# The substitution steps of a chunked gated DeltaNet issued from GpSimd, and the first heads' gated rows issued two ticks later

## The chip, the cores and the metric

The kernel runs on one core of one Trainium2 chip. A core has a matrix engine (TensorE, PE in the profile), VectorE (DVE), ScalarE (ACT), GpSimd (POOL) and SyncE (SP), which here only issues DMA transfers. Each engine takes its instructions in the order in which they were queued for it, and waits for the others by semaphores. The metric is the device time of one execution in microseconds (us), of which the median over several runs is given. All data are float32.

## The reference

Two layers of a hybrid decoder for 256 tokens of width 1024: a half feed-forward block, a token mixer, a cross-attention into 256 memory tokens, another half feed-forward block. In the first layer the mixer is attention beside a linear recurrence; in the second, to which the change belongs, it is a chunked gated delta rule with 8 heads of width 128. Cut to what matters:

```python
def gated_delta_rule_chunked(q, k, v, g, beta):
    ...
    kkt = einsum('bhnid,bhnjd->bhnij', k * beta[..., None], k) * decay
    amat = eye(C) + where(strict, kkt, 0.0)
    rhs = concatenate([v * beta[..., None], k * beta[..., None] * exp(gcum)[..., None]], axis=-1)
    sol = triangular_solve(amat, rhs, left_side=True, lower=True, unit_diagonal=True)
    ...
    o = rmsnorm(o, o_norm) * silu(z)
    return o.reshape(B, S, W) @ w_out
```

So for every head and chunk of tokens a unit lower triangular system is solved, and the rows of the result are normalised and gated by silu(z) before the output projection.

## The kernel before

The activations lie transposed in SBUF: 8 tiles of 128 features x 256 tokens. Every weight tile is loaded by SP (`raw`, L141, 512 KB, five buffers), copied by ACT (L158) and its rounding rest formed by DVE (L159); the pair of halves, `wt`, is what PE multiplies, in two passes (L200 and L204, or L216 and L220 where tokens are the rows of the result). The products gather in PSUM banks named psw (3), pss (3) and psf (2). DVE and ACT bring them out: `add` (L270 on ACT, L271 on DVE) gives `xn` or `z`.

In `mixer1` the order of the projections is DN_ORDER: keys, queries, values and gates of the four pairs of heads (k0, q0, v0, z0 and so on). Each projected pair goes through a convolution of four taps (L1078, and three L1081 on DVE), a SiLU and its own further steps. Small pieces of work are hung into the sequence by `after(n, fn)`: they are emitted n ticks later, a tick being about a quarter of a projection. This fixes the order of the program as it is written. From it a list scheduler with its own estimates of the durations makes the queue of each engine; it may let a later instruction pass an earlier one, and it keeps the data dependences. So the place of an instruction in a queue follows from what the scheduler expects of the time of the others.

The kernel solves the triangular system by inverting it. The 128 x 128 matrix of a head and chunk of 128 tokens (`na`, L1176, on DVE) is stored to DRAM (L1180), and its 16 x 16 diagonal blocks are read back with one block per partition (`nb`, L1235): 64 blocks for the two pairs of one group. There are two groups: heads 0 to 3 and heads 4 to 7. `invert(g)` then does the substitution inside the blocks, in 15 steps of two instructions:

```python
def step(j):
    n, m = 15 - j, j + 1
    nc.vector.tensor_mul(tm[:, :n, :m], nb[:, j, m:, None]..., ti[:, 0, j:m, :m]...)   # L1240
    nc.vector.tensor_add(ti[:, 0, m:, :m], ti[:, 0, m:, :m], tm[:, :n, :m])            # L1242
    if j == 14:
        nc.vector.tensor_copy(ti[:, 1], ti[:, 0].rearrange("p a b -> p b a"))          # L1244
```

A step works on 64 partitions and (15-j) x (j+1) elements of each, 15 to 64. Each instruction needs the one before it. `ti[:, 0]` and its transpose `ti[:, 1]` are stored (L1248, SP) and loaded again as 128 x 128 matrices `tu` (L1254, SP). `tu`, `nb` and `ti` have one buffer each, shared by the two groups. `back(p)` goes on from the blocks of 16 to 128 by products on PE (L1275, L1281, L1287), with a masked copy on DVE in each of three rounds (L1282), and then computes the result of the head pair. `gated(p)` multiplies the result by its norm and gate (L1346, DVE), and `gated_T(p)` transposes it (L1355, PE) and splits it (L1356 on ACT, L1357 on DVE) into `a2`, which the output projection reads.

GpSimd has, in this part, the power -1/2 of the norms (L341), of which `rs_dn` is read by DVE at L1202 (`rq_all`) and at L1153 (`hb_all`).

Of the kernel before, what the change touches and what calls it, by code (L numbers as in the profile page):

```python
# [67 lines left out]
class Net:  # L68
# [939 lines left out]
    def mixer1(self, mid, kT_mem, mem_mov, gnext):  # L1008
        nc, tc, t = self.nc, self.tc, self.t
# [3 lines left out]
        with tc.tile_pool(name="m1", bufs=1, reuse_waits="tile") as mp:  # L1013
# [213 lines left out]
            def invert(g):  # L1227

                d0, d1 = self.d0[g], self.d1[g]
                nb = mp.tile([64, 16, 16], F32, name="nb", bufs=1)  # L1230
                ti = mp.tile([64, 2, 16, 16], F32, name="ti", bufs=1)
                tm = mp.tile([64, 16, 16], F32, name="tm", bufs=1)
                tu = mp.tile([P, 2, 2, 4, P], F32, name="tu", bufs=1)
                def load():
                    nc.sync.dma_start(nb, at(d0, 0, [[DB, 64], [P, 16], [1, 16]]))  # L1235
                    nc.vector.tensor_copy(ti[:, 0], self.eye16)

                def step(j):
                    n, m = 15 - j, j + 1
                    nc.vector.tensor_mul(tm[:, :n, :m], nb[:, j, m:, None].to_broadcast([64, n, m]),  # L1240
                                         ti[:, 0, j:m, :m].to_broadcast([64, n, m]))
                    nc.vector.tensor_add(ti[:, 0, m:, :m], ti[:, 0, m:, :m], tm[:, :n, :m])  # L1242
                    if j == 14:
                        nc.vector.tensor_copy(ti[:, 1], ti[:, 0].rearrange("p a b -> p b a"))  # L1244

                def store():
                    for i in range(2):
                        nc.sync.dma_start(at(d1, i * 8 * DH, [[DB, 64], [P, 16], [1, 16]]), ti[:, i])  # L1248

                def spread():  # L1250
                    for q in range(2):
                        st[2 * g + q]["tu"] = tu[:, :, q]
                        for i in range(2):
                            nc.sync.dma_start(tu[:, i, q], at(d1, (8 * i + 4 * q) * DH, [[P, P], [DH, 4], [1, P]]))  # L1254

                t0, t1, t2, t3 = INV
                assert t0 <= t1 and t1 + 4 <= t2 < t3
                self.after(t0, load)
                for j in range(15):
                    self.after(t1 + j // 3, lambda j=j: step(j))  # L1260
                self.after(t2, store)
                self.after(t3, spread)
# [78 lines left out]
            def gated(p):  # L1341
                o, z = st[p]["o"], st[p].pop("z")
                for j in range(2):
                    for c in range(2):
                        i = 2 * j + c
                        nc.vector.scalar_tensor_tensor(o[:, i], o[:, i], ro_all[:, c, 2 * p + j:2 * p + j + 1],  # L1346
                                                       z[:, c, j * P:j * P + P], op0=OP.mult, op1=OP.mult)

            def gated_T(p):
                o = st[p].pop("o")  # L1350
                hs = slice(2 * p, 2 * p + 2)
                po = self.bank("s")
                for j in range(2):
                    for c in range(2):
                        nc.tensor.transpose(po[:, j, tok(c)], o[:, 2 * j + c], self.ident)  # L1355
                nc.scalar.activation(a2[:, hs, 0], po, AF.Copy, scale=onorm)  # L1356
                nc.vector.scalar_tensor_tensor(a2[:, hs, 1], po, onorm, a2[:, hs, 0].bitcast(F32),  # L1357
                                               op0=OP.mult, op1=OP.subtract)
# [3 lines left out]
            def unit(step):  # L1362
                kind, c = step[0], int(step[1])
                if kind == "K":
                    yield from self.mem_key(c, mem_mov, kT_mem)
                    return
                if kind == "z":
                    z = mp.tile([P, 2, S], F32, name="z", bufs=2)
                    yield from self.unit_t("dn_w_in", 3072 + c * 256, mov, self.to(z))
                    nc.scalar.activation(z, z, AF.Silu)  # L1370
                    st[c]["z"] = z
                    return
                a = "qkv".index(kind)
                y = mp.tile([P, 2, S], F32, name="y", bufs=YB)
                yield from self.unit("dn_w_in", a * 1024 + c * 256, mov,
                                     lambda j, ps: conv(y, j, a * 8 + 2 * c + j, ps))
                twice = 2 if step in TWICE else 1
                silu(y, twice)
                if kind == "k":
                    yks[c] = y  # L1380
                    key_steps(c, y, NK[c], twice)
                elif kind == "q":
                    query_steps(c, yks.pop(c), y, twice)
                else:
                    value_steps(c, y, twice)
# [7 lines left out]
            for i, part in enumerate(DN_ORDER):  # L1393
                if i % 2 == 0:
                    for step in part.split():
                        self.run(unit(step))
                    continue
                group, bg = part.split("|")
                gens = [back(int(p)) for p in group]
                bg = deque(unit(step) for step in bg.split())  # L1400
                parts = list(DN_FILL[i // 2])
                if i == 1:
                    self.fill(bg, 2)
                while gens:
                    gens = [g_ for g_ in gens if next(g_, 0) is None]
                    if gens:
                        self.fill(bg, parts.pop(0))
                if i == 1:
                    self.fill(bg)
                    for n, p in enumerate(group):  # L1410
                        self.after(1 + n, lambda p=int(p): gated(p))
                        self.after(4 + n, lambda p=int(p): gated_T(p))
                    continue
                for p in group:
                    gated(int(p))
                for p in group:
                    self.fill(bg, parts.pop(0))
                    gated_T(int(p))
                self.fill(bg)
# [81 lines left out]
```

## Time and profile before

| | us |
|---|---|
| median of 3 runs | 1252.54 (1251.08 to 1254.22) |
| profiled execution: its own time | 1250.74 |
| profiled execution: span | 1249.0 |
| busy in the span: PE | 1235.7 |
| busy: DVE | 929.3 |
| busy: ACT | 751.8 |
| busy: POOL | 80.9 |

The span is what the profiler sees between the first and the last instruction; 1.7 us of the execution lie outside it. Times in the rows below are counted from the start of the span. A row of the timeline gives the start, the duration, the engine, the line of the code, the operation and what it writes and reads; in brackets stands how long the engine was idle before it, and what ended that. A row of a line or tile gives the shortest, the median and the longest duration in ns. The start of the next instruction on an engine may come a little before the end of the last, since they overlap in part. The change lies between about 820 and 915 us of the span.

### The profile page before, as it was taken

Reading aid. Unit: us, or ns where it says so; the run is one execution under the profiler, and the core shown is the slowest. Engines: PE = TensorE matmul, PEld = TensorE weight load, DVE = VectorE, ACT = ScalarE, POOL = GpSimd, SP = SyncE. Lnnn points to the kernel's source line nnn. Section 1 sums busy time; section 2 is a strip of 40 time slices with the busy share of each in tenths; the row PEclk is TensorE's granted clock in tenths of the full one; section 3 lists DMA queues with packets and bytes.
Section 4 is the critical chain, followed back from the end, with each engine's and each line's share of the span. In section 5 each row is a group of like instructions: output and inputs, shape, how many; then the busy total and the mean of one; then the engine's idle time right before and its main releaser. Section 6 shows DMA issues by size and latency. Waiting matters only on the chain.

```text
span 1249.0 us, 20308 instructions
## 1 busy us (share of the span) xinstructions
PE 1235.7 (99%) x7702; PEld 1105.1 (88%) x7702; DVE 929.3 (74%) x1594; ACT 751.8 (60%) x1281; POOL 80.9 (6%) x97
## 2 busy tenths in 40 slices
PE   9999999999999999999999999999999999999998
PEld 8888889888998888888888888888898998888887
DVE  6987957788668778766877756989757668777753
ACT  7766545886555665545666544776757555665543
POOL 1000020000101000011000001020001101000000
PEclk9999999999999999999999999999999999999999
DMA  8766575534544565556656566667533545566552
GB/s 272 215 208 197 185 254 185 177 128 151 187 135 153 185 195 184 187 183 229 188 185 198 175 193 206 189 150 197 140 102 132 178 131 165 185 190 188 177 188 72
DMA packets 231018, 222.92 MB, mean 178 GB/s; under 512 B 14968, under 2 KB 228616, under 8 KB 230792
## 3 DMA queue, kind: packets, MB, share of 16 engines
q1 hardware_dynamic: 229448, 217.94, 55.9%
q0 software_dynamic: 1152, 3.15, 1.0%
q8 instruction: 60, 0.98, 0.3%
q10 hardware_dynamic: 320, 0.53, 0.1%
q14 instruction: 38, 0.31, 0.1%
HBM read 215.03 MB, written 5.51 MB: 177 GB/s over the span
## 4 chain that ended last, share of the span: by engine, by line
PE 90%; DVE 5%; ACT 2%; DMA 1%; issue 1%; POOL 1%; ACTq 0%; DVEq 0%; POOLq 0%
PE psw L200 21%; PE pss L200 16%; PE psw L204 11%; PE psf L200 11%; PE pss L204 8%; PE psf L204 5%; PE psw L242 5%; PE psf L242 4%; PE pss L242 3%; PE psw L216 2%; DVE wt L159 1%; PE psw L220 1%; ACT wt L158 1%; PE pss L1275 1%; PE psf L1281 1%
## 5 line engine op out<-in xcount | busy, mean ns | idle before, releaser
L159 DVE TENSOR_TENSOR wt<-raw,wt 128x1024 fp32r<-128x1024 f32 (+1 forms) x409 | 484.6, 1190 | 203.3 <-ACT wt L158 200.5
L158 ACT ACTIVATE wt<-raw 128x1024 fp32r<-128x1024 f32 (+1 forms) x409 | 418.6, 1031 | 172.3 <-PE psw L204 59.4
L200 PE MATMUL psw<-x,wt 128*128 128x512 f32 x864 | 310.6, 396 | 1.7 <-DVE xn L271 1.5
L204 PE MATMUL psw<-x,wt 128*128 128x256 f32 x864 | 224.9, 281 | 0.5 <-DVE wt L159 0.5
L200 PE MATMUL pss<-x,wt 128*128 128x512 f32 x520 | 187.4, 393 | 0.0
L200 PEld LDWEIGHTS psw<-x,wt 128*128 128x128 f32 x864 | 160.6, 188 | 29.7 <-issue 1.7
L204 PEld LDWEIGHTS psw<-x,wt 128*128 128x128 f32 x864 | 162.5, 188 | 9.4 <-DVE wt L159 1.0
L204 PE MATMUL pss<-x,wt 128*128 128x256 f32 x520 | 134.9, 280 | 0.0
L200 PE MATMUL psf<-x,wt 128*128 128x512 f32 x352 | 127.2, 394 | 0.0
L200 PEld LDWEIGHTS pss<-x,wt 128*128 128x128 f32 x520 | 97.7, 188 | 16.9 <-ACT bc L377 0.4
L204 PEld LDWEIGHTS pss<-x,wt 128*128 128x128 f32 x520 | 97.7, 188 | 5.4
L200 PE MATMUL psw<-h,wt 128*128 128x512 f32 x264 | 94.9, 396 | 0.0
L204 PE MATMUL psf<-x,wt 128*128 128x256 f32 x352 | 91.3, 280 | 0.0
L200 PE MATMUL pss<-h,wt 128*128 128x512 f32 x242 | 87.0, 396 | 0.0
L336 POOL TENSOR_TENSOR acc<-acc,sq 128x256 f32<-128x256 f32 x49 | 43.7, 891 | 658.5 <-ACT sq L334 557.5
L200 PEld LDWEIGHTS psf<-x,wt 128*128 128x128 f32 x352 | 66.1, 188 | 11.2
L204 PE MATMUL psw<-h,wt 128*128 128x256 f32 x264 | 72.0, 280 | 0.0
L204 PEld LDWEIGHTS psf<-x,wt 128*128 128x128 f32 x352 | 66.2, 188 | 3.5
L204 PE MATMUL pss<-h,wt 128*128 128x256 f32 x242 | 66.0, 280 | 0.0
L200 PEld LDWEIGHTS psw<-h,wt 128*128 128x128 f32 x264 | 49.6, 188 | 10.8
L200 PE MATMUL psf<-h,wt 128*128 128x512 f32 x154 | 55.4, 397 | 0.0
L200 PEld LDWEIGHTS pss<-h,wt 128*128 128x128 f32 x242 | 45.5, 188 | 9.8
(385 smaller groups left out, 2108.9 us busy)
## 6 DMA issues: line engine op xcount, KB each, us to landing
raw<-in_ffn_w_in_dram SPq DMA_DIRECT2D x175, 512.0 KB, 3.6
raw<-in_ffn_w_out_dram SPq DMA_DIRECT2D x80, 512.0 KB, 3.5
raw<-in_xa_wkv_dram SPq DMA_DIRECT2D x32, 512.0 KB, 3.4
raw<-in_dn_w_in_dram SPq DMA_DIRECT2D x32, 512.0 KB, 4.0
raw<-in_ab_w_in_dram SPq DMA_DIRECT2D x20, 512.0 KB, 3.5
raw<-in_xa_wq_dram SPq DMA_DIRECT2D x16, 512.0 KB, 3.5
raw<-in_xa_wo_dram SPq DMA_DIRECT2D x16, 512.0 KB, 3.3
raw<-in_ffn_w_out_dram SPq DMA_DIRECT2D x16, 256.0 KB, 2.7
```

The source lines that it names most:

```text
L158: nc.scalar.activation(a, r, AF.Copy)
L159: nc.vector.tensor_sub(b, r, a.bitcast(F32))
L200: nc.tensor.matmul(out.rearrange("p a s -> p (a s)"), w[:, 0, cols], mov[:, k].rearrange("p a s -> p (a s)"), start=k == start, stop=k == ...
L204: nc.tensor.matmul(out[:, 0], w[:, 1, cols], mov[:, k, 0], start=False, stop=False)
L216: nc.tensor.matmul(out.rearrange("p a s -> p (a s)"), mov[:, k, 0, tok], w.rearrange("p a s -> p (a s)"), start=k == 0, stop=k == KD - 1)
L220: nc.tensor.matmul(out[:, 0], mov[:, k, 1, tok], w[:, 0], start=False, stop=False)
L242: self.nc.tensor.matmul(out, a[u], b[w], start=first and i == 0, stop=last and i == 2)
L336: (eng or nc.gpsimd).tensor_add(self.acc, self.acc, sq)
L1275: nc.tensor.matmul(py[:, i], na[:, i], tu[:, 0, i], start=True, stop=True)
L1281: nc.tensor.matmul(pp[:, i], yy[:, i], tu[:, 1, i], start=True, stop=True)
```

## The change

```diff
                 def step(j):
                     n, m = 15 - j, j + 1
-                    nc.vector.tensor_mul(tm[:, :n, :m], nb[:, j, m:, None].to_broadcast([64, n, m]),
+                    nc.gpsimd.tensor_mul(tm[:, :n, :m], nb[:, j, m:, None].to_broadcast([64, n, m]),
                                          ti[:, 0, j:m, :m].to_broadcast([64, n, m]))
-                    nc.vector.tensor_add(ti[:, 0, m:, :m], ti[:, 0, m:, :m], tm[:, :n, :m])
+                    nc.gpsimd.tensor_add(ti[:, 0, m:, :m], ti[:, 0, m:, :m], tm[:, :n, :m])
                     if j == 14:
                         nc.vector.tensor_copy(ti[:, 1], ti[:, 0].rearrange("p a b -> p b a"))
...
                 if i == 1:
                     self.fill(bg)
                     for n, p in enumerate(group):
-                        self.after(1 + n, lambda p=int(p): gated(p))
-                        self.after(4 + n, lambda p=int(p): gated_T(p))
+                        self.after(2 + n, lambda p=int(p): gated(p))
+                        self.after(6 + n, lambda p=int(p): gated_T(p))
                     continue
```

The 30 instructions of a group's substitution go to GpSimd; the copy that transposes the result stays on VectorE, and the tile `eye` is still copied into `ti` there. The gated rows of heads 0 to 3 are emitted one tick later, and their transposes two ticks later. The arithmetic is the same.

The scheduler makes new queues from this. On GpSimd, at the end of the first group's steps (`tm_8397` and `ti_8396` are its tiles; a number tells one tile from the next of the same name), there now stands:

```order
L1240 TENSOR_TENSOR tm_8397<-nb_8395,ti_8396 64x2x14
L1242 TENSOR_TENSOR ti_8396<-ti_8396,tm_8397 64x2x14
L1240 TENSOR_TENSOR tm_8397<-nb_8395,ti_8396 64x15
L1242 TENSOR_TENSOR ti_8396<-ti_8396,tm_8397 64x15
L341 TENSOR_TENSOR rs_dn_8529<-ss_8527,mhalf_88 128x4
L341 TENSOR_TENSOR rs_dn_8589<-ss_8587,mhalf_88 128x4
```

All 30 steps stand in one piece, and the two powers that VectorE reads at L1202 and L1153 stand behind them.

On VectorE, in the first group, the difference of the queues where these powers are read (`xn_8602` is the second half of the fourth key projection, `wt_8632` holds weights of the first gate projection):

```order
 L1151 RECIPROCAL r2_8591<-ss_8587 128x4
+L1153 TENSOR_TENSOR hb_all_7943<-ss_8587,rs_dn_8589 128x2x2
+L1081 SCALAR_TENSOR_TENSOR y_8503<-xn_8550,dcw_91,y_8503 128x253
+L1152 TENSOR_TENSOR nb_all_7942<-nbeta_7935,r2_8591 128x2x2
 L271 TENSOR_TENSOR xn_8602<-psw_8567,xn_8602 128x256
-L1240 TENSOR_TENSOR tm_8397<-nb_8395,ti_8396 64x8x8
-L1152 TENSOR_TENSOR nb_all_7942<-nbeta_7935,r2_8591 128x2x2
-L1153 TENSOR_TENSOR hb_all_7943<-ss_8587,rs_dn_8589 128x2x2
-L1242 TENSOR_TENSOR ti_8396<-ti_8396,tm_8397 64x8x8
+L1244 COPY ti_8396<-ti_8396 64x256
 L159 TENSOR_TENSOR wt_8632<-raw_8403,wt_8632 128x4x256
```

Before, the queue was in the middle of the substitution here, with 14 of the 30 instructions to come after this piece. Now `hb_all` stands ahead of the evacuation `xn_8602`, and the transposing copy L1244 directly behind it, ahead of the weight split. A few rows further up, the L1202 that reads `rs_dn_8529` stands in both queues, ahead of this piece.

On VectorE, in the second group (`ti_8848` and `tm_8849`; `tu_8398` belongs to heads 0 to 3), before:

```order
L1242 TENSOR_TENSOR ti_8848<-ti_8848,tm_8849 64x12x4
L271 TENSOR_TENSOR z_8891<-psw_8896,z_8891 128x256
L1240 TENSOR_TENSOR tm_8849<-nb_8847,ti_8848 64x11x5
L1282 COPY_PREDICATED tu_8398<-dn_m5_1681,psf_8947 128x512
L1242 TENSOR_TENSOR ti_8848<-ti_8848,tm_8849 64x11x5
```

and with the change:

```order
L1081 SCALAR_TENSOR_TENSOR y_8778<-xn_8871,dcw_91,y_8778 128x253
L1244 COPY ti_8848<-ti_8848 64x256
L271 TENSOR_TENSOR z_8891<-psw_8896,z_8891 128x256
L1282 COPY_PREDICATED tu_8398<-dn_m5_1681,psf_8947 128x512
L1282 COPY_PREDICATED tu_8398<-dn_m5_1681,psf_8953 128x512
```

The steps are gone from between the evacuation and the masked copies, and the transposing copy L1244, which stood behind all of them, stands ahead of them.

On SP the first store L1248 and the loads L1254 of the first group stand between raw loads that they followed before, and in the second group both L1248 stand two raw loads earlier. On PE the transposes L1355 of the first pair of heads, which stood just ahead of the first products L1275 of heads 4 to 7, stand behind the products L1281 of the first round of these heads.

## Prediction

> **What bounds the kernel now.** I read the page first: shares of the engines, then the chain that ended last.
>
> ```profile
> PE 1235.7 (99%) x7702; PEld 1105.1 (88%) x7702; DVE 929.3 (74%) x1594; ACT 751.8 (60%) x1281; POOL 80.9 (6%) x97
> PE 90%; DVE 5%; ACT 2%; DMA 1%; issue 1%; POOL 1%; ACTq 0%; DVEq 0%; POOLq 0%
> ```
>
> TensorE (PE) is busy for 1235.7 of 1249.0 us, so all that any change outside it can win is about 13 us of its idle time, while any wait it is newly given adds to the end one for one. Next I asked which waits of PE belong to the places that the change touches (the view of waits, PE alone: total, times, longest).
>
> ```profile
> PE pss L1355 <- DVE qk L1346: 1.0, 1, 1.0
> PE psw L216 <- DVE tm L1240: 0.4, 1, 0.4
> PE pss L1287 <- DVE tu L1282: 0.4, 1, 0.4
> PE psw L216 <- DVE xn L271: 0.3, 1, 0.3
> ```
>
> These four, 2.1 us together, are the whole prize near the substitution and the gated rows. They also say that VectorE (DVE) and PE run here with almost no slack: whatever is late on DVE is late on PE. The timeline of the two engines shows it in both groups. The first group (heads 0 to 3), DVE and then PE:
>
> ```profile
> 831.39 0.16 DVE L1202 TENSOR_SCALAR rq_all<-rs_dn 128x4 f32<-128x4 f32 x1
> 831.46 0.17 DVE L1240 TENSOR_TENSOR tm<-nb,ti 64x15 f32<-64x15 f32 x1
> ...
> 836.31 0.19 DVE L1240 TENSOR_TENSOR tm<-nb,ti 64x48 f32<-64x48 f32 x1
> 836.43 0.48 DVE L1081 SCALAR_TENSOR_TENSOR y<-xn,dcw,y 128x254 f32<-128x254 f32 x1
> 836.83 0.20 DVE L1242 TENSOR_TENSOR ti<-ti,tm 64x48 f32<-64x48 f32 x1
> ...
> 840.38 0.15 DVE L1113 TENSOR_SCALAR ss<-pss 128x4 f32<-128x4 f32 x1
> ...
> 840.67 0.40 DVE L271 TENSOR_TENSOR xn<-psw,xn 128x256 f32<-128x256 f32 x1
> ...
> 841.72 0.16 DVE L1153 TENSOR_TENSOR hb_all<-ss,rs_dn 128x4 f32<-128x4 f32 x1 [0.45 <-POOL rs_dn L341]
> ...
> 841.94 1.21 DVE L159 TENSOR_TENSOR wt<-raw,wt 128x1024 fp32r<-128x1024 f32 x1
> 843.07 0.21 DVE L1240 TENSOR_TENSOR tm<-nb,ti 64x63 f32<-64x63 f32 x1
> ...
> 851.01 0.38 DVE L1244 COPY ti<-ti 64x256 f32<-64x256 f32 x1
> ```
> ```profile
> 843.29 0.47 PE L216 MATMUL psw<-wt,x 128*128 128x512 f32 x1 [0.40 <-DVE tm L1240]
> ```
>
> The weight split L159 ends at 843.15, and PE, which needs that tile, starts at 843.29 after 0.40 of waiting. From start to next start a step holds DVE for 0.12 us (836.31 to 836.43), an L1081 for 0.40, an L159 for 1.13. The second group:
>
> ```profile
> 867.01 0.18 DVE L1240 TENSOR_TENSOR tm<-nb,ti 64x15 f32<-64x15 f32 x1 [1.19 <-DMA nb<-d]
> ...
> 868.67 0.41 DVE L271 TENSOR_TENSOR z<-psw,z 128x256 f32<-128x256 f32 x1
> ...
> 869.13 0.72 DVE L1282 COPY_PREDICATED tu<-dn_m,psf 128x512 f32<-128x512 uint8 x1
> ...
> 870.87 0.71 DVE L1282 COPY_PREDICATED tu<-dn_m,psf 128x512 f32<-128x512 uint8 x1
> ...
> 877.47 0.37 DVE L1244 COPY ti<-ti 64x256 f32<-64x256 f32 x1
> ```
> ```profile
> 871.64 0.66 PE L1287 MATMUL pss<-ident,tu 128*128 128x128 f32 x4 [0.38 <-DVE tu L1282]
> ```
>
> Today the masked copies L1282 of heads 0 to 3, on which PE waits, are slipped between the steps of heads 4 to 7.
>
> **What one step costs on GpSimd (POOL).** It is not in this trace; the nearest rows, with the DVE row it replaces:
>
> ```profile
> L1240 DVE TENSOR_TENSOR tm<-nb,ti x30: 156/199/218, 831.5 to 877.1; 64x15 f32<-64x15 f32 x4, 64x28 f32<-64x28 f32 x4, 64x39 f32<-64x39 f32 x4, 64x48 f32<-64x48 f32 x4
> L336 POOL TENSOR_TENSOR acc<-acc,sq x49: 732/787/1395, 154.3 to 1058.5; 128x256 f32<-128x256 f32 x49
> L1488 POOL MEMSET const-uint8-127<- 128x1 uint8 x1 | 0.1, 113 | 0.0
> 840.67 1.01 POOL L341 TENSOR_TENSOR rs_dn<-ss,mhalf 128x4 f32<-128x4 f32 x1 [5.44 <-DVE ti L1242]
> ```
>
> A group is 30 instructions (15 products, 15 sums), each waiting for the one before. Their lengths are (15-j)(j+1), 45 elements on average. From below, each costs as the one-element MEMSET does, 0.11 us, and 0.03 for the hand-over: a group takes T = 4.2 us. From above, each costs the 0.73 of the 256-element sum and 0.05: T = 23; the 1.01 of L341 is a power, not a sum, and counts only as a far limit. On the line from 0.11 at one element to 0.73 at 256 (2.4 ns each), 45 elements are 0.22; with 0.05 of hand-over 0.27. A product opens two reads and short rows, which a MEMSET doesn't, so I take 0.30, near the lower end because 45 elements lie nearer to one than to 256: **T = 9.0 us**. The Trainium skill, "GPSIMD Engine Reference", section 3.1, has ordinary two-input arithmetic at 1.96 times VectorE's time; an estimate by that ratio from the 0.199 above is 0.39 and 0.05 of hand-over, T = 13.2, and the sum below would be 1273; no run has shown that ratio yet.
>
> A second price is the turns the two engines take. L323, a VectorE operation with two operands in SBUF, beside a POOL sum:
>
> ```profile
> 966.67 0.47 DVE L323 SCALAR_TENSOR_TENSOR x<-xT,prm,x 128x256 fp32r<-128x256 f32 x1
> 967.80 1.22 DVE L159 TENSOR_TENSOR wt<-raw,wt 128x1024 fp32r<-128x1024 f32 x1 [0.66 <-ACT wt L158]
> 968.61 1.01 POOL L336 TENSOR_TENSOR acc<-acc,sq 128x256 f32<-128x256 f32 x1 [0.87 <-ACT sq L334]
> 968.94 0.96 DVE L323 SCALAR_TENSOR_TENSOR x<-xT,prm,x 128x256 fp32r<-128x256 f32 x1
> ```
>
> L336 starts inside an L159, takes 1.01 instead of 0.73 and ends at 969.62; the L323 behind it, 0.47 when alone, ends only at 969.90. They run one after the other, so a POOL step loses what such a DVE operation still takes.
>
> **First group: the change adds two waits on DVE.** In the new order the power rs_dn (L341) stands behind all 30 steps in POOL's queue, and DVE waits for it at rq_all (L1202), then for the next power at hb_all (L1153), then for the last step at the copy L1244. Behind these stand the evacuation L271, and the split L159 for which PE waits. The first nb load has landed by 831.46, when DVE uses it; I start POOL at 831.5. Until DVE reaches that rq_all it issues two L159 and six L1081, all with two SBUF operands: 2 x 1.13 + 6 x 0.40 = 4.7 us of turns; I put down 4.6. Without these T would be 9.0, with all of them 13.6; I take all, since POOL always has a next step. POOL ends at 845.1. Then 1.0 (first power), 0.1 (rq_all), 1.34 from L1113 to hb_all (840.38 to 841.72 above: the second power), 0.5 (hb_all, an L1081, nb_all), 0.7 (L271 and L1244, each under 0.4 to the next start), 1.2 (L159) and 0.14 to PE: 5.0 us, PE starts at 850.1 instead of 843.29: **+6.8 us**. The DVE time that is given back (the 14 later instructions at 0.12 each) hides nothing, as PE has already been held; it only lets DVE catch up.
>
> ```profile
> 849.97 0.61 SPq L1248 DMA_DIRECT2D d<-ti  x1
> ...
> 852.63 1.24 SPq L1254 DMA_DIRECT2D tu<-d  x2
> ```
> ```profile
> 857.24 1.95 PE L1275 MATMUL pss<-tu,na 128*128 128x128 f32 x16
> ```
>
> On SP the stores L1248 and the loads L1254 are pulled ahead of raw loads, and the first L1248 now waits for POOL. In the old run 7.3 us lie between the store and the product L1275 that needs it. With POOL done at 845.1 the product could start at about 852.4; PE in the new order reaches it 14 matmuls earlier than at the old 857.24, but 6.8 us later on the clock: covered, cost nothing. If POOL took 9 us longer, PE would have been held longer too by the first wait, so this never decides. The raw loads behind L1248 lose about 5 us of lead, and the splits that read them are 6.8 later: nothing.
>
> **Second group: the copy L1244 now stands ahead of L1282.** All 30 steps leave DVE, and L1244, which needs the last, stays where the scheduler thought POOL would be done: ahead of L271 and both L1282. DVE is idle here, so POOL has the memory alone, T = 9.0. In old times (all shifted by the first delay) nb lands at 867.0 and POOL ends at 876.0. Add 0.7 for L1244 and L271, 1.3 for two L1282 and 0.1 to PE: PE starts its second L1287 at 878.1 instead of 871.64: **+6.5 us**. The result itself is not hurried: tu of heads 4 to 7 is loaded only when the tu of heads 0 to 3 is free (one buffer), long after (the L1254 quoted below).
>
> **Gated rows later.** The same 8 + 8 instructions, no DMA.
>
> ```profile
> 900.49 0.68 PE L1355 MATMUL pss<-ident,qk 128*128 128x128 f32 x3
> 902.17 0.33 PE L1355 MATMUL pss<-ident,qk 128*128 128x128 f32 x1 [0.99 <-DVE qk L1346]
> 902.33 1.96 PE L1275 MATMUL pss<-tu,na 128*128 128x128 f32 x16
> ```
> ```profile
> 891.95 2.03 SPq L1254 DMA_DIRECT2D tu<-d  x4
> ```
> ```profile
> tu<-d SPq DMA_DIRECT2D x8, 256.0 KB, 4.5
> ```
>
> The transposes move behind the L1281 of heads 4 to 7, and L1275 takes their place; its tu is issued from 891.95 to 893.98 and lands 4.5 us after, by 898.5, so it is there. The 0.99 us wait goes: **-1.0 us** (at worst 0, if L1110 behind L1275 then waits for its squares). They stay far from the output projection, whatever the change's title says.
>
> **The sum** against the profiled execution's own 1250.74 us: +6.8 + 6.5 - 1.0 = +12.3, so 1263.1; its 1250.74 is 1.8 under the median of the three runs, 1252.54, so I predict **1265 us**. In T: the change is about 2T - 5.7.
>
> **Rivals.**
> (1) *GpSimd about as quick as VectorE.* For: MEMSET's 0.11, and the substitution is small. Against: L336's 0.73 for 256 elements, and the turns. With T = 4.2 the change is +2.7: 1255. It decides below T = 4.7 (0.16 us a step).
> (2) *Each step costs nearly a whole L336.* For: sums over short rows and broadcast operands have no row here. With 0.5 a step T = 15, +24: 1277; with 0.73, T = 23, +40: 1293. The ratio of the Trainium skill's page would put it between this and mine.
> (3) *The other side: VectorE's relief reaches PE.* 30 steps of about 0.12 us leave its queue per group, and if POOL has finished before DVE comes to L1202 and L1244, all four waits go: -2.1, 1250.4. 2T - 5.7 turns negative only below T = 2.9, under 0.1 us a step, less than any row of POOL. To be faster by more than it can be told, PE would also have to lose waits elsewhere.
> (4) *The change doesn't do what it says:* L1244 stays on VectorE, so the substitution isn't off its queue but a wait in it. This is my forecast's own ground; were the order on the chip other than the one shown, the case would be (3).
>
> **Chances.** Forecast (T from 5 to 14) 0.72, rival 1 0.11, rival 2 0.13, rival 3 with 4 0.04. A measurement tells about 0.3% of this kernel, 3.8 us, from no change. Rival 1 and most of rival 3 are "same"; so faster 0.03, same 0.12, slower 0.85. The range runs from rival 1's 1255 to rival 2's 1277.
>
> **What would show it.** Right: L1240 and L1242 on POOL at 0.2 to 0.4 us, longer in the first group than in the second; DVE idle before L1202 or L1153 (released by POOL rs_dn) and before L1244 (released by POOL ti) in each group for some 5 us and more; PE waiting on DVE at L216 and at L1287 for about 6 us each; no wait at L1355. Wrong: POOL done before DVE arrives, PE idle near 13 us as before; or the loss elsewhere, at L1275 behind the tu loads or in the splits behind the raw loads.

## The result, and the profile after

The changed kernel takes 1264.82 us (median of 4 executions, 1264.66 to 1265.81), the kernel before 1253.37 (1251.08 to 1254.22): a ratio of 1.0096, 95% interval 1.0078 to 1.0113. It is 11.4 us slower; 1265 was forecast. The profiled execution took 1265.81 us with a span of 1264.0, so 15.1 more than the profiled one of before. First the page of the changed kernel, shares of the engines and the chain that ended last, then the waits of TensorE (PE) in the part that changed (total, times, longest):

```profile
PE 1239.7 (98%) x7702; PEld 1107.8 (88%) x7702; DVE 921.5 (73%) x1534; ACT 750.9 (59%) x1281; POOL 100.9 (8%) x157
PE 87%; DVE 4%; POOL 2%; DMA 2%; ACT 2%; issue 2%; SPq 0%; ACTq 0%; POOLq 0%; DVEq 0%
```
```profile
PE psw L216 <- ACT wt L158: 5.7, 1, 5.7
PE pss L1287 <- DVE tu L1282: 5.1, 1, 5.1
...
PE psf L1281 <- issue: 0.8, 1, 0.8
```

PE is idle 24.3 us instead of 13.3. It is also *busy* 4.0 us longer, with the same 7702 matmuls: some of them ran slower. The two long waits stand at the places that the prediction named; L1355 is gone from the list, and a wait at L1281 has come. The first wait carries the name of ACT's L158, but the timeline of the first group shows what came last, VectorE's split L159, which ends at 848.60, 0.15 us ahead of PE:

```profile
830.20 0.97 POOL L1240 TENSOR_TENSOR tm<-nb,ti 64x15 f32<-64x15 f32 x1 [1.91 <-DMA nb<-d]
...
831.68 1.16 POOL L1240 TENSOR_TENSOR tm<-nb,ti 64x28 f32<-64x28 f32 x1
...
836.78 1.18 POOL L1242 TENSOR_TENSOR ti<-ti,tm 64x63 f32<-64x63 f32 x1
...
843.48 0.21 POOL L1242 TENSOR_TENSOR ti<-ti,tm 64x15 f32<-64x15 f32 x1
843.66 1.01 POOL L341 TENSOR_TENSOR rs_dn<-ss,mhalf 128x4 f32<-128x4 f32 x1
...
844.70 0.17 DVE L1202 TENSOR_SCALAR rq_all<-rs_dn 128x4 f32<-128x4 f32 x1 [6.02 <-POOL rs_dn L341]
...
847.11 0.36 DVE L1244 COPY ti<-ti 64x256 f32<-64x256 f32 x1
847.39 1.21 DVE L159 TENSOR_TENSOR wt<-raw,wt 128x1024 fp32r<-128x1024 f32 x1
...
848.75 0.77 PE L216 MATMUL psw<-wt,x 128*128 128x512 f32 x1 [5.74 <-ACT wt L158]
849.31 0.41 PE L220 MATMUL psw<-wt,x 128*128 128x256 f32 x1
849.52 0.63 PE L216 MATMUL psw<-wt,x 128*128 128x512 f32 x1
```

GpSimd (POOL) does its 30 steps from 830.20 to 843.69, then the power; VectorE (DVE) stands 6.02 us before L1202, and PE starts 5.46 us later than before (843.29). The second group:

```profile
871.25 0.22 POOL L1240 TENSOR_TENSOR tm<-nb,ti 64x15 f32<-64x15 f32 x1 [10.23 <-DMA nb<-d]
...
881.86 0.21 POOL L1242 TENSOR_TENSOR ti<-ti,tm 64x15 f32<-64x15 f32 x1
...
882.11 0.37 DVE L1244 COPY ti<-ti 64x256 f32<-64x256 f32 x1 [9.34 <-POOL ti L1242]
...
883.50 1.97 PE L1287 MATMUL pss<-ident,tu 128*128 128x128 f32 x8 [5.13 <-DVE tu L1282]
```

DVE stands 9.34 us before the copy L1244, and behind it wait the masked copies. The steps themselves, by line (shortest, median, longest in ns):

```profile
L1240 POOL TENSOR_TENSOR tm<-nb,ti x30: 208/276/1162, 830.2 to 881.6; 64x15 f32<-64x15 f32 x4, 64x28 f32<-64x28 f32 x4, 64x39 f32<-64x39 f32 x4, 64x48 f32<-64x48 f32 x4
L1242 POOL TENSOR_TENSOR ti<-ti,tm x30: 213/308/1184, 831.3 to 881.9; 64x15 f32<-64x15 f32 x4, 64x28 f32<-64x28 f32 x4, 64x39 f32<-64x39 f32 x4, 64x48 f32<-64x48 f32 x4
```

The slower matmuls stand in the view by windows of 2 us around the first stop (busy us of PE, PEld, DVE, ACT, POOL; then the granted PE clock, DMA share, GB/s):

```profile
844.00:846.00 2.00, 0.00 (x0) 0.00 (x0) 0.71 (x4) 0.00 (x0) 1.66 (x2) 1.00 0.31 33
846.00:848.00 2.00, 0.00 (x0) 0.00 (x0) 1.77 (x6) 1.10 (x3) 0.19 (x1) 0.87 0.28 82
848.00:850.00 2.00, 1.25 (x4) 1.09 (x5) 2.00 (x5) 2.00 (x3) 0.00 (x0) 0.50 1.01 279
850.00:852.00 2.00, 2.00 (x8) 1.71 (x7) 2.00 (x5) 0.68 (x3) 0.00 (x0) 0.50 1.20 301
852.00:854.00 2.00, 2.00 (x8) 1.71 (x7) 2.00 (x7) 0.77 (x2) 0.00 (x0) 0.50 0.51 167
854.00:856.00 2.00, 2.00 (x13) 1.65 (x13) 0.93 (x1) 1.21 (x4) 0.00 (x0) 0.92 0.95 257
```

The granted clock falls to half while PE stands and stays there. Taken as full or half, the means put half clock from 847.5 to 854.3, 6.8 us; 5.6 of them are behind the stop. A pair L216, L220 starts every 0.64 us there (849.52 to 850.16) instead of every 0.35. The same happens behind the second stop. PE's delay against before grows so. It is 5.46 us at L216 (the first stop). At L1287 it is 12.45: 870.67 to 883.50, less the 0.38 that PE of before has yet to wait there. The second stop gives 4.75 of this (5.13 less 0.38), so PE was 7.7 late ahead of it, 2.2 of which came from half clock. It is 14.6 at L1294 (2.2 from half clock), 14.5 behind the gated rows and 15.0 at the end.

### The profile page after: what moved, and what is told of

It reads as the page before. It is cut to its first block, busy times and chain, and to the rows that moved or that the text cites. A ratio compares the mean times of both kernels' runs of the same rounds, so it can differ in the third digit from the quotient of the medians.

```text
span 1264.0 us, 20311 instructions
## 1 busy us (share of the span) xinstructions
PE 1239.7 (98%) x7702; PEld 1107.8 (88%) x7702; DVE 921.5 (73%) x1534; ACT 750.9 (59%) x1281; POOL 100.9 (8%) x157
## 4 chain that ended last, share of the span: by engine, by line
PE 87%; DVE 4%; POOL 2%; DMA 2%; ACT 2%; issue 2%; SPq 0%; ACTq 0%; POOLq 0%; DVEq 0%
PE psw L200 20%; PE pss L200 15%; PE psw L204 10%; PE psf L200 10%; PE pss L204 8%; PE psf L204 5%; PE psw L242 4%; PE psf L242 4%; PE pss L242 2%; PE psw L216 2%; DVE wt L159 1%; PE psw L220 1%; POOL ti L1242 1%; POOL tm L1240 1%; ACT wt L158 1%
## 5 line engine op out<-in xcount | busy, mean ns | idle before, releaser
L159 DVE TENSOR_TENSOR wt<-raw,wt 128x1024 fp32r<-128x1024 f32 (+1 forms) x409 | 484.7, 1190 | 203.2 <-ACT wt L158 200.5
L158 ACT ACTIVATE wt<-raw 128x1024 fp32r<-128x1024 f32 (+1 forms) x409 | 418.3, 1031 | 173.1 <-PE psw L204 58.9
L204 PE MATMUL psw<-x,wt 128*128 128x256 f32 x864 | 224.7, 280 | 1.3 <-DVE wt L159 1.3
L204 PEld LDWEIGHTS psw<-x,wt 128*128 128x128 f32 x864 | 162.5, 188 | 10.3 <-DVE wt L159 1.9
L204 PE MATMUL pss<-x,wt 128*128 128x256 f32 x520 | 134.9, 280 | 0.0
L204 PEld LDWEIGHTS pss<-x,wt 128*128 128x128 f32 x520 | 97.7, 188 | 5.3
L204 PE MATMUL psf<-x,wt 128*128 128x256 f32 x352 | 91.3, 280 | 0.0
L204 PE MATMUL psw<-h,wt 128*128 128x256 f32 x264 | 72.0, 280 | 0.0
L204 PEld LDWEIGHTS psf<-x,wt 128*128 128x128 f32 x352 | 66.2, 188 | 3.5
L204 PE MATMUL pss<-h,wt 128*128 128x256 f32 x242 | 66.0, 280 | 0.0
L200 PEld LDWEIGHTS psw<-h,wt 128*128 128x128 f32 x264 | 49.6, 188 | 10.8
```

What stands on the lines that cost most here:

```text
L158: nc.scalar.activation(a, r, AF.Copy)
L159: nc.vector.tensor_sub(b, r, a.bitcast(F32))
L200: nc.tensor.matmul(out.rearrange("p a s -> p (a s)"), w[:, 0, cols], mov[:, k].rearrange("p a s -> p (a s)"), start=k == start, stop=k == ...
L204: nc.tensor.matmul(out[:, 0], w[:, 1, cols], mov[:, k, 0], start=False, stop=False)
```

## The experiments

My theory was: (a) DVE's queue stands twice behind the end of the steps, first by the powers, then by L1244; (b) each stop of PE is followed by half clock at about 2.2 us; (c) the gated rows are worth nothing. The rivals were DVE and GpSimd shutting each other out of the memory, and a loss in SP's order or in the gated rows.

**The two halves of the change apart.** `step_only`:

```diff
-                        self.after(2 + n, lambda p=int(p): gated(p))
-                        self.after(6 + n, lambda p=int(p): gated_T(p))
+                        self.after(1 + n, lambda p=int(p): gated(p))
+                        self.after(4 + n, lambda p=int(p): gated_T(p))
```

> Only the substitution goes to GpSimd; the gated rows stay where they were before. Theory (VectorE stands in its queue behind GpSimd twice, and TensorE runs at half clock after each stop): in the profile after, the shift of TensorE against before was 14.6 us when it came to the gated rows and 14.5 behind them, so the gated rows are worth 0.1 us: this kernel takes the time of the change as a whole, 1264.8, within 1 us. Rival as the prediction had it (the gated rows win 1.0): 1265.8. Rival: the gated rows are themselves part of the loss, through the order the scheduler makes of them: under 1262.

`gated_only` is the kernel before with the reverse of this edit.

> Only the gated rows move; the substitution stays on VectorE. Theory: the 0.99 us wait of TensorE before L1355 goes, and a wait of about 0.8 us comes at the product L1281, as in the profile after: no difference, 1253.4 within 0.8 us. Rival as the prediction had it: -1.0 us, 1252.4, with no wait in the other place. Rival: moving the rows costs by itself: over 1255.

`step_only` took 1267.72 (1264.45 to 1270.04), ratio 1.0117 (1.0098 to 1.0137): the whole loss, and 3 us more than I expected of the median. Its profiled execution, 1264.45, has the same two stops (6.0 and 5.7 us) and a 1.0 us wait at L1355; the higher executions have no profile. The two highest have a lower mean granted clock than the profiled one (0.990 and 0.992 against 0.994), so part of their excess is more half clock; the 1267.72 has 0.993, as one of 1264.56 has, and its 3 us stay unexplained. `gated_only` took 1253.3, ratio 1.0001 (0.999 to 1.0013): the gated rows are worth nothing that shows, and 1.6 us at most. The wait at L1355 is gone and a wait of 0.8 us at L1281 has come, as expected. But its profiled execution took 1254.25, 3.5 more than that of before, and shows why with no work of this change near it (first PE's delay, then the windows):

```profile
820.26 0.47 PE L200 MATMUL psw<-x,wt 128*128 128x512 f32 x1 [1.98 <-DVE xn L271]
...
836.40 1.06 PE L1204 MATMUL psf<-y 128*128 128x128 f32 x8
```
```profile
820.00:822.00 2.00, 1.74 (x10) 1.54 (x10) 1.39 (x6) 2.00 (x7) 0.00 (x0) 0.87 1.09 245
822.00:824.00 2.00, 2.00 (x11) 2.00 (x11) 2.00 (x7) 2.00 (x4) 0.00 (x0) 0.50 0.63 184
824.00:826.00 2.00, 2.00 (x11) 1.90 (x10) 2.00 (x4) 2.00 (x7) 0.00 (x0) 0.50 0.44 129
```

At about 819 PE waits 1.5 to 2.4 us in every profile of this study, because ScalarE stands before the exponential L1132 for a load. In the kernel before:

```profile
817.07 0.99 ACT L1132 ACTIVATE e<-e,ngc 128x128 f32<-128x128 f32 x3 [3.57 <-DMA e<-gd]
```
```profile
820.17 0.47 PE L200 MATMUL psw<-x,wt 128*128 128x512 f32 x1 [1.45 <-DVE xn L271]
...
833.13 1.06 PE L1204 MATMUL psf<-y 128*128 128x128 f32 x8
```

There no half clock follows. In `gated_only` it follows a stop of 1.98 us, and PE, 0.1 us late at 820, is 3.3 us late at L1204. So half clock needs no GpSimd, and single profiles may differ by 3 us through it alone.

**One group at a time.** In both, the engine of L1240 and L1242 is chosen by the group:

```diff
-                    nc.gpsimd.tensor_mul(...)
+                    (nc.gpsimd if g == 0 else nc.vector).tensor_mul(...)   # group1_only; g == 1 for group2_only; L1242 alike
```

> Only heads 0 to 3 have their substitution on GpSimd, heads 4 to 7 on VectorE as before. Theory: the first stop of the change as a whole and nothing else: TensorE waits 5.5 us at L216 for the powers behind the steps, then 5.5 to 6 us at a granted clock of 0.50, which cost 2.2: +7.7 us, 1261. If the half clock were an accident of that one profile: +5.5, 1259. Rival: the loss comes from the second group alone, or from GpSimd and VectorE taking turns at the memory all over: under 1256.

> Only heads 4 to 7 have their substitution on GpSimd. Here the scheduler puts the transposing copy L1244 behind the two masked copies L1282 and ahead of a weight split L159, not ahead of the masked copies. Theory: the nb load lands at 867.0 as before, 30 steps take 10.8 us, GpSimd ends at 877.8, the copy and the split end at 879.4, where the split of before was done by about 874: TensorE waits about 5 us, now at L216 for that split and not at L1287, then about 2.2 us are lost at half clock: +7 us, 1260.5 (+4 to +9). Rival (the place in the queue doesn't matter, L1287 is held by the memory or the masks): a wait at L1287 again of 5 us. Rival: a second group without the first costs nothing: within 2 us of before.

1257.56, ratio 1.004 (1.0025 to 1.0055), and 1257.55, ratio 1.0037 (1.0022 to 1.0051). Each group alone costs about 4 us, less than the 7 I expected of each. The two stand for 8 of the 11.4 us of the change; the rest isn't accounted for, and the second group alone has another queue than in the change. For the first, PE's wait at L216 is 2.9 us and not 5.5:

```profile
849.09 0.77 PE L216 MATMUL psw<-wt,x 128*128 128x512 f32 x1 [2.94 <-ACT wt L158]
```

This execution had half clock already behind the stop at 819. PE came to L216 about 3 us later, GpSimd did not, and the wait is shorter by as much: a stop and an earlier loss at half clock don't add. For the second, DVE stands 6.49 us before L1244, but the two masked copies are ahead of it here:

```profile
879.34 0.37 DVE L1244 COPY ti<-ti 64x256 f32<-64x256 f32 x1 [6.49 <-POOL ti L1242]
```
```profile
882.38 2.08 PE L1281 MATMUL psf<-tu,yy 128*128 128x128 f32 x8 [3.25 <-ACT yy L1277]
```

PE goes through L1287 without a wait and stops 3.25 us later on, at L1281, and not at L216, where I had put it. The way there is in the timeline: behind L1244 stood an evacuation L271, for which ScalarE waited ahead of L1370, and behind that stood the L1277 that PE needed:

```profile
881.21 0.63 ACT L1370 ACTIVATE z<-z 128x512 f32<-128x512 f32 x1 [4.29 <-DVE z L271]
```

The loss is set by what stands *behind* the waiting instruction in the queue: the rival that the place doesn't matter falls.

**The copy on other engines.** `copy_pool` and `copy_act`:

```diff
-                        nc.vector.tensor_copy(ti[:, 1], ti[:, 0].rearrange("p a b -> p b a"))
+                        nc.gpsimd.tensor_copy(ti[:, 1], ti[:, 0].rearrange("p a b -> p b a"))               # copy_pool
+                        nc.scalar.activation(ti[:, 1], ti[:, 0].rearrange("p a b -> p b a"), AF.Copy)       # copy_act
```

> The change, with the transposing copy L1244 also on GpSimd: VectorE has nothing left that waits for the last step. The two powers of the first group still stand behind all 30 steps. Theory: the stop of the second group goes (TensorE at L1287 waits under 1 us, no half clock behind it), the one of the first stays at 5.5 us and 2.2 of half clock: 1264.8 - 6.9 = 1258 to 1261. Rival (what holds VectorE in the second group is not L1244 but the shared memory): 1264 to 1266. Rival (the copy is dear on GpSimd and holds the powers and the store): over 1266.

> The change, with the transposing copy L1244 on ScalarE. In ScalarE's queue the copy stands ahead of an L1078 and two L158 in the first group, ahead of an L158 and two L1288 in the second. Theory (any engine whose queue holds an instruction that needs the last step is held until GpSimd ends, and TensorE with it): ScalarE is idle some 5 to 9 us before L1244 in the second group, TensorE waits 4 to 7 us for tu of L1288 or for a split, and half clock follows: 1262 to 1267, no better than the change. Rival (it is VectorE alone, by its memory port): the second stop goes, 1258 to 1260, as with the copy on GpSimd.

`copy_pool` took 1258.86, ratio 1.0044 (1.0031 to 1.0058): the second stop is gone, as expected, and the first remains (3.4 us). Its profiled execution, 1264.49, is the slowest of its seven and has half clock in two places more, near the start (behind a stop of 3.9 us) and behind the stop that the other profiles have at 819; as in `group1_only`, half clock ahead of L216 goes with a shorter wait there. `copy_act` took 1265.86, ratio 1.0103 (1.0088 to 1.0118): no better than the change. ScalarE now stands, and PE behind it:

```profile
884.48 0.63 ACT L1244 ACTIVATE ti<-ti 64x256 f32<-64x256 f32 x1 [8.73 <-POOL ti L1242]
```
```profile
886.59 3.79 PE L1275 MATMUL pss<-tu,na 128*128 128x128 f32 x16 [6.29 <-ACT tu L1288]
```

It isn't DVE and its memory: any engine that keeps its order and holds an instruction that needs the last step stands until GpSimd is done.

**A longer stop.** `double_mul` does each product of the second group twice:

```diff
-                    nc.gpsimd.tensor_mul(tm[:, :n, :m], ...)
+                    for _ in range(1 + g): nc.gpsimd.tensor_mul(tm[:, :n, :m], ...)
```

> The change, with every product L1240 of the second group done twice (the same values): 15 more instructions of about 0.36 us from start to start on GpSimd, 5.4 us. The scheduler puts L1244 between the two masked copies here, ahead of the second. Theory (VectorE's queue waits for the end of the steps, and the half clock behind a stop is of one length, whatever the stop's): TensorE's wait at L1287 grows from 5.1 to about 10, the half clock behind it stays at 5.5 to 7 us: 1264.8 + 5 = 1270. Rival (the half clock grows with the stop): 1272 and more. Rival (the steps are hidden, and the second stop is of another making): 1265.

1269.05, ratio 1.0124 (1.0107 to 1.0141): 4.2 us more than the change, where I had 5. The wait at L1287 is 9.4 us (expected about 10). The half clock did not follow as I wrote it:

```profile
882.00:884.00 2.00, 0.00 (x0) 0.00 (x0) 0.00 (x0) 0.00 (x0) 1.53 (x7) 0.90 0.00 0
884.00:886.00 2.00, 0.00 (x0) 0.00 (x0) 0.00 (x0) 0.00 (x0) 1.52 (x7) 0.50 0.00 0
886.00:888.00 2.00, 0.34 (x2) 0.34 (x3) 1.40 (x3) 0.00 (x0) 0.42 (x2) 0.50 0.05 6
888.00:890.00 2.00, 2.00 (x9) 1.81 (x8) 0.70 (x1) 0.60 (x1) 0.00 (x0) 0.50 0.71 75
890.00:892.00 2.00, 2.00 (x16) 1.86 (x15) 0.42 (x1) 0.98 (x2) 0.00 (x0) 0.89 0.82 238
```

It lasts 6.8 us again (883.6 to 890.4), but from its fall, which comes in the middle of the stop; only the part behind 887.66, 2.8 us, meets any work. In this profile the longer stop paid *less* behind it.

**Both stops taken away.** `pow_first`, `pow_split` and `pow_early` have the copy on GpSimd and let the two powers in among the steps of the first group. A small copy of `rs_dn` into `tm` makes a step wait for a power. In `pow_split` (`self.rs` holds the last two powers that were emitted):

```diff
-                    n, m = 15 - j, j + 1
+                    n, m = 15 - j, j + 1; g == 0 and j in (7, 11) and nc.gpsimd.tensor_copy(tm[:, 0, :4], self.rs[j // 4 - 3][:64])
...
-                    self.after(t1 + j // 3, lambda j=j: step(j))
+                    self.after(t1 + (j * 8 // 14 if g == 0 else j // 3), lambda j=j: step(j))
```

`pow_first` has both powers ahead of the eighth step, `pow_early` has them ahead of the eighth and the ninth.

> As copy_pool, and in the first group the steps from the eighth on are emitted later and made to wait (a small copy of rs_dn into tm ahead of the eighth step) for the two powers, which so stand in the middle of the steps on GpSimd. Theory: both stops go; VectorE waits for rs_dn at most as long as one step and one power take, under 1.5 us; GpSimd ends the first group at about 848 to 850, and the store is as early as before (849.9): TensorE idle 12 to 14 us and no half clock: 1251 to 1255, the time of before within 0.2%. Rival (GpSimd beside VectorE slows both, stops or not): 1257 to 1262. Rival (the relief of VectorE by 30 steps a group reaches TensorE): under 1250.

> As pow_first, but the two powers are let in at two places: the first ahead of the eighth step, the second ahead of the twelfth, so that GpSimd does not stand still between them. In pow_first the stop at L216 was gone, but GpSimd ended the first group at 852.6 and TensorE waited 2.95 and 1.42 us at L1275 for tu, with half clock behind. Theory: here GpSimd ends at 847 to 849, earlier than the store of before at 849.97, so L1275 doesn't wait; the second power comes at most 1 us late; no stop of TensorE over 1.5 us in the two groups, and no half clock there: the time of before, 1252 to 1255. Rival (GpSimd beside VectorE is dear by itself, wherever the waits are): 1257 and more, with the waits spread over many places. Rival (VectorE's relief is worth something once the waits are gone): under 1251.

> As pow_split, but the second power is let in ahead of the ninth step instead of the twelfth. In pow_split its input was there at 839.2, four steps more were done first, VectorE waited 3.73 us for it at L1153 and TensorE 3.27 us at L216, with no half clock behind; the executions lay together at 1253.7 to 1255.1. Theory: the power comes about 2.5 to 3 us earlier, TensorE's stop at L216 falls under 0.8 us, GpSimd ends the group no later than 849: the profile, where it has no half clock, is 1250 to 1252 as before, the median 1251 to 1254: no difference from the kernel before, or 0.1 to 0.2% faster. Rival (what is left of the stop is not the power's place): a wait of 3 us at L216 again, 1254. Rival (VectorE's relief is worth something once no wait is left): under 1250.

`pow_first` missed: 1257.94, ratio 1.0043 (1.0028 to 1.0058). The stop at L216 is gone, but GpSimd stood for the second power, its steps ended late, and the wait went to the next in line, the loads of `tu`:

```profile
842.27 1.18 POOL L341 TENSOR_TENSOR rs_dn<-ss,mhalf 128x4 f32<-128x4 f32 x1 [3.52 <-DVE ss L1113]
```
```profile
860.78 1.16 PE L1275 MATMUL pss<-tu,na 128*128 128x128 f32 x8 [2.95 <-DMA tu<-d]
```

`pow_split` took 1254.05, ratio 1.0004 (0.9993 to 1.0014), the time of before. One stop was still there, which I had not expected, 3.27 us long and with no half clock behind it:

```profile
843.53 0.16 DVE L1153 TENSOR_TENSOR hb_all<-ss,rs_dn 128x4 f32<-128x4 f32 x1 [3.73 <-POOL rs_dn L341]
```
```profile
845.84 0.47 PE L216 MATMUL psw<-wt,x 128*128 128x512 f32 x1 [3.27 <-DVE wt L159]
```

`pow_early` took that wait down to about 1 us, and won nothing by it: 1254.64, ratio 1.0005 (0.999 to 1.0021). Its profiled execution, 1255.96, has no half clock, and 1250 to 1252 was expected of it. Its waits of PE (the 1.9 at L204 is near the start, at 30 us, away from the change):

```profile
PE pss L1275 <- DMA tu<-d: 2.4, 2, 1.3
PE psw L204 <- DVE wt L159: 2.4, 2, 1.9
...
PE psw L216 <- DVE wt L159: 1.5, 2, 1.0
```

GpSimd ended the group at 851.0, not by 849 as I had written, and the wait is at `tu` again.

Taking 60 steps off DVE wins nothing: none of these kernels is faster than before. That GpSimd beside DVE costs nothing is less sure than the medians say, since they mix executions with and without half clock. The mean granted clock is on record for every execution, and a stretch of 6.8 us at half clock lowers it by 0.0027 (half of 6.8 in 1249 us). The kernel before ran 80 times beside the experiments. The 33 executions with a clock of 0.999 or more took 1250.4 to 1253.8 us (median 1251.4). Nine of the twelve of `pow_early` have such a clock, and they took 1253.5 to 1256.0 (median 1254.4). So about 3 us are left, which the medians hide because `pow_early` had half clock less often. In its profile PE is idle 18.1 us against 13.3 before and busy 0.4 longer, so what is left there is waits.

**The stop at 819.** `exp_late` is the kernel before with `EXP = (17, 18, 22, 23)` for `(16, 17, 22, 23)`; `split_exp` is that edit in `pow_split`.

> The kernel before, with nothing of the change; only the exponentials L1132 of heads 0 and 1 are emitted one tick later, so that ScalarE brings out a projection (L270) before it waits for the load e. In the profiles so far TensorE stops 1.45 to 2.4 us at about 819, because ScalarE stands before L1132 for that load, and in 5 of 9 profiles, of kernels with and without GpSimd, the granted clock was 0.50 for 3 to 7 us behind it. Theory (a stop of TensorE of this length halves the clock in some executions and not in others, and this is the spread of the runs): without the stop no half clock near 820, and the runs lie together near the lowest of before: 1248 to 1251, spread under 2 us. Rival (half clock comes at this place whatever TensorE does): spread as before, 1251 to 1256, with half clock near 820 in the profile or not.

> pow_split and exp_late together. Theory: both stops of the change are gone and the one at 819 too: as exp_late, 1248 to 1252, faster than both kernels by 2 to 5 us; the substitution on GpSimd itself is worth nothing, since TensorE has no wait left that it could take away. Rival (relief of VectorE counts): 1 to 2 us under exp_late. Rival (GpSimd beside VectorE costs): over exp_late by more than 2.

1255.07, ratio 1.0013 (1.0 to 1.0025), and 1255.31, ratio 1.0016 (1.0006 to 1.0026). The edit failed at its aim: ScalarE still stands 3.9 us before L1132 in `exp_late` and 4.3 in `split_exp`, the stop of PE is still there, and half clock behind it in both profiles:

```profile
819.93 0.64 PE L200 MATMUL psw<-x,wt 128*128 128x512 f32 x1 [1.80 <-DVE xn L271]
```

So the runs do not show what the kernel would take without this stop. That the spread of the executions is half clock can be read from the granted clocks, though: against the 33 executions of before at 0.999 or more (median 1251.4 us), the 38 at 0.997 or less took 1253.7 to 1261.0 (median 1254.8); nine lie between. The 3.4 us between the medians are half of 6.8. Where the half clock lies in executions without a profile isn't on record; the stop at 819 is the longest that the profile of before has, so that it is this one is likely, not shown. No version beat the kernel before.

## Why the prediction was right, and where it was not

The forecast named the two places, the two mechanisms and the time. The time, though, owes something to errors that cancelled.

- **T, a group's steps alone.** I took 0.30 a step from start to start, 9.0 us, of which 0.25 was the instruction. The second group, beside a DVE that did three L1081 at its start and then stood, took 871.25 to 882.07: 10.8 us, 0.36 a step, of which the three L1081 cost some 0.5 us in all. Both parts were too small: the instructions took 0.276 and 0.308 at the median, and the hand-over from one to the next some 0.07 to 0.08, not 0.05. The Trainium skill, "GPSIMD Engine Reference", section 3.1, has 1.96 times VectorE's time, for 2048 elements. The trace doesn't agree for operations this short: 0.276 against 0.199 is 1.4.
- **Turns.** I put 4.6 us for all the operations of DVE with two operands in SBUF; the first group took 13.5 against 10.8, so 2.7. The three steps that start inside a weight split L159 were long (0.97, 1.16, 1.18). Those beside an L1081 took 0.25 to 0.38, so they lost at most 0.14 us each, where I had charged the L1081's whole 0.40. T too small and the turns too dear gave 13.6 for 13.5: two errors that cancelled.
- **First group, +6.8.** Measured +5.46. The chain from GpSimd's end to PE was right (5.06 for 5.0). The start was off by 1.3 us: `nb` was there by 830.20; 831.5 was when DVE had come to use it. Of the three waits that I named on DVE, the one at L1244 did not come in this group: the powers behind the steps held DVE past their end.
- **SP and the loads of tu, nothing.** Right: no wait at L1275. `pow_first` shows the cover's end: when GpSimd finished about 9 us later, at 852.6, the wait was there.
- **Second group, +6.5.** Measured +4.75, though T was longer. The step that failed is "all shifted by the first delay": PE came 7.7 us late, but `nb` only 4.25 late (867.0 to 871.25), so part of the second wait was spent while PE was still behind from the first. The end to PE took 1.43, not 2.1: it is the first L1287 that waits now, and it needs one masked copy, not two.
- **Gated rows, -1.0.** Measured -0.1. The 0.99 went as said, and 0.8 came at L1281, which now stands ahead of the transposes; I had looked only at L1110 behind them. The profile names no releaser for it.
- **Half clock, not in the sum.** About 4.4 us, two times 2.2. The prediction priced a wait of PE at its length.

So 6.8 + 6.5 - 1.0 = 12.3 stood against 5.46 + 4.75 - 0.1 + 4.4 + 0.5 = 15.0 in the profiled execution (the 0.5 came behind the gated rows): what the stops lacked, half clock more than made up. Of the medians the difference is 11.4. That it is less than 15 has a reason on record: the profiled execution of before, at a clock of 0.999, is one without the half clock of 6.8 us, and the profiled one of the change is the longest of its four. Against the 1251.4 of the executions of before without that half clock, the change's median is 13.4 longer. So the forecast of 1265 met the time partly because it was added to a median that had some half clock in it.

Of the rivals, the first (GpSimd as quick as DVE) and the second (0.5 a step and more) fell by the 0.36. The third, that DVE's relief reaches PE, fell with `pow_split` and `pow_early`: no time is won even with the waits mostly gone, though some 3 us of them were left. The fourth held in its own sense: `copy_pool` shows that leaving L1244 on DVE was about half the loss.

## What to carry to other kernels

Moving a chain of small operations to an idle engine doesn't take it off the other's queue as long as one reader of its end stays there: look for the readers (here a copy and two powers), and for what stands behind them. When a wait is removed, name the next consumer in line; here it was `tu`, and the gain ended there. Where PE is the bound, price a stop of several us at its length and 2 to 3 us more, and don't add the prices of two stops, since the second starts from a PE that is already late. Where executions of one kernel spread, sort them by their granted clock before you compare medians.

## What the hardware did that I had not expected

**Half clock.** Behind every stop of PE of 5 us and more in the changed part (5.1 to 9.4 us, in four profiles) the granted clock was 0.50 for 6.8 us, counted from its fall, 2.3 to 5.3 us after PE had stopped. Shorter stops differ. Behind 2.94 and 3.25 us there were 3.4 us of it, behind 3.37 (`copy_pool`) and behind 2.95 with 1.42 close after it (`pow_first`) 6.8, and behind the 3.27 of `pow_split` none. Of 14 profiles with a stop of 1.45 to 2.4 us at 819, seven show it (the shortest stop 1.80 us) and seven don't (the longest 2.38). It cost 2.2 us behind the first stop of the change and 3.2 where PE had no other wait (`gated_only`).

The traces show more of what decides. In each profile the times at which the granted clock changes are whole multiples of 3.41 us apart (in the changed kernel 2, 8 and 2 of them). Cut into windows on this grid, the 14 profiles have 20 falls to half up to 1240 us (one more comes at the end of each). PE was busy for 47% or less of the window just ahead of each. Of the other windows at full clock only three were under 50%, at 44, 45 and 49.8%. So it is the share of a window that counts: the 1.80 us stop of `exp_late` lay in one window (47% busy), the 3.27 us of `pow_split` in two (50 and 54%). Why half clock lasted one window three times and two the other times isn't shown. The Trainium skill, "TensorE: Matmul & The Clock Gate", part 1, has a free-running window of about 3.4 us and half clock after an idle one, and gives as rule that PE should have no idle gaps over about 3.4 us. The window and the lengths, 3.4 and twice that, agree. The limit does not: 1.80 us was enough in one profile here, and 3.27 not in another.

**Turns at the memory.** A GpSimd step that starts inside an L159 ends 0.1 to 0.2 us behind it (831.68 to 832.84, the L159 from 831.54 to 832.75). With an L1081, which has two operands in SBUF as well, it is the same (871.91 to 872.34, the L1081 from 871.77 to 872.25), only that far less of it is left to wait for: this step took 0.43, where one of its size alone took 0.23. An L1081 that starts with a step or just behind one took 0.57 or 0.61 instead of 0.47. The Trainium skill, "SBUF — State Buffer", section "Who interferes with whom", has VectorE instructions with two SBUF inputs contend with GpSimd ones that read SBUF; the trace agrees for L159 and for L1081.
